# A two-layer decoder trunk: last down product by PSUM bank, final norm in halves

## The chip, the cores and the metric

The kernel runs as one program on one core of a Trainium2 chip. The metric is the device time of one execution in microseconds. The kernel before takes 1856.09 us, the median of three runs (1855.35 to 1857.3).

## The reference

The computation is a causal two-layer decoder trunk on 256 tokens of width 2048, all in float32. Each layer has a token mixer (a pooling mixer in layer 0, differential attention in layer 1) and a SwiGLU feed-forward block, each behind a root-mean-square norm and with a residual addition. A last norm gives the output.

```python
def rmsnorm(x, g, eps=RMS_EPS):
    xf = x.astype(jnp.float32)
    y = xf * lax.rsqrt(jnp.mean(xf * xf, axis=-1, keepdims=True) + eps)
    return (y * g.astype(jnp.float32)).astype(x.dtype)

def swiglu(h, wg, wu, wd):
    return (jax.nn.silu(h @ wg) * (h @ wu)) @ wd

    for i in range(DEPTH):
        ...
        h = h + mix
        h = h + swiglu(rmsnorm(h, norm_ffn[i]), w_gate[i], w_up[i], w_down[i])
    return rmsnorm(h, final_norm)
```

The change touches only the end of the second layer: the last part of the product with `w_down`, its residual addition, and the final `rmsnorm`. The norm needs the sum of squares over all 2048 columns of a token before any column of that token can be scaled.

## The kernel before

**Tiling.** The residual `x_tok` stays in SBUF as two token blocks of 128 rows (t = 0 and 1) by 2048 columns. Weights come in chunks of 1 MB: a `raw` tile of four blocks of 128x512, loaded from SyncE's DMA queue (`load`, L111). ScalarE rounds a chunk to its high half `whi` and VectorE subtracts to get its low half `wlo` (`halves`, L116 to L121). Each float32 product is made of three matmuls, high by high, high by low and low by high (L179). The pools for `raw` and for the halves hold three chunks each.

**A group.** `group` (L142) takes a list of steps, one chunk of weights each, and adds all of them up in PSUM banks. Some steps use a seven-product scheme; the last group of the program uses none (L385: `by_seven` is empty), so each of its six steps has 24 matmuls, six for each of four banks. The banks are C11 (bank 6), C12 (bank 4), C21 (bank 5) and C22 (bank 7); the first digit is the token block and the second the column block of 512. The loop at L158 makes a step's halves and then all of its products, so the steps follow one another and each step visits the four banks in the order C11, C12, C21, C22.

**The feed-forward block.** `ffn` (L351) runs over the hidden dimension in parts of 4, 4 and 3 slices (`CHUNKS`). After each part it multiplies by `w_down`, once for each half `o` of the 2048 output columns. The group of the last part, second layer and o = 1 is the last one of the program: its four banks are the last quarter-columns 1024 to 2047 of both token blocks.

**The end.** For the last group the banks are taken in the order of L389, C11, C12, C21, C22. For each one VectorE adds the bank to the residual (L392), ScalarE squares the 512 new columns with a running sum (L221, the sums in `ss_next`), and VectorE multiplies by the norm's gain into a tile `y` (L398). Behind a token block's second bank, a sum over its four partial sums (L405) and a short chain of 128x1 operations (`rsqrt`, L205: one square root on ScalarE, five small operations on VectorE) give the token's factor. Then the block's four `y` pieces of 512 columns are scaled, two on ScalarE (L408) and two on VectorE (L409), and two DMAs of 512 KB each write 1024 columns each, the first from SyncE's queue, the second from ScalarE's (L410).

**What sets the order.** Each engine has its own queue and works in order. The order within a queue is set at build time by a scheduler of the language's tile layer, from the order in which the program is written and its own costs; waits between engines are semaphores.

Of the kernel before, what the change touches and what calls it, by code (L numbers as in the profile page):

```python
# [9 lines left out]
F32 = mybir.dt.float32  # L10
F32R = mybir.dt.float32r
AF = mybir.ActivationFunctionType
ALU = mybir.AluOpType
AX = mybir.AxisListType
PSUM = bass.MemoryType.PSUM

P = 128
S = 256
D = 2048
# [21 lines left out]
SEVEN_DOWN = (2, 4, 6)  # L41
# [6 lines left out]
A22, A21, A11, A12, S1, S3, S2, S4 = range(8)  # L48
# [4 lines left out]
def trunk_kernel(ctx, tc, x_n, gains, scale_in, final_in, subln, lam_in, band, dist,  # L53
# [10 lines left out]
    nc = tc.nc  # L64
# [5 lines left out]
    tmp = ctx.enter_context(tc.tile_pool(name="tmp", bufs=2))  # L70
# [4 lines left out]
    def bank(i, shape=(P, 512)):  # L75
        return psum.tile(list(shape), F32, name=f"b{i}", tag=f"b{i}")
# [54 lines left out]
    def sum_halves(pool, t):  # L131
        hi = pool.tile([P, 4, 512], F32R, name="thi")
        lo = pool.tile([P, 4, 512], F32R, name="tlo")
        nc.scalar.copy(hi, t)  # L134
        nc.vector.tensor_tensor(lo, t, f32(hi), ALU.subtract)  # L135
        return hi, lo
# [2 lines left out]
    M1, M6, M7, P5, P3, P4, M2, X = range(8)  # L139
    C11, C12, C21, C22 = M2, P3, P4, X  # L140

    def group(steps, pool):  # L142


        plan = []
        for a, seven, src in steps:
            if seven:
                plan.append([(M1, [(A11, 0, B11)]), (M2, [(A12, 0, B21)]), (M6, [(S2, 1, T2)]), (M7, [(S3, 1, T3)]),
                             (P5, [(S1, 1, T1)]), (P3, [(S4, 0, B22)]), (P4, [(A22, 1, T4)])])
            else:  # L150
                plan.append([(C11, [((0, 0), 0, B11), ((1, 0), 0, B21)]), (C12, [((0, 0), 0, B12), ((1, 0), 0, B22)]),
                             (C21, [((0, 1), 0, B11), ((1, 1), 0, B21)]), (C22, [((0, 1), 0, B12), ((1, 1), 0, B22)])])
        left = {}
        for step in plan:
            for b, parts in step:
                left[b] = left.get(b, 0) + 3 * len(parts)
        ps = {}
        for (a, seven, src), step in zip(steps, plan):  # L158
            raw = load(src)
            t = sums(pool, raw) if seven else None  # L160
            w = [halves(raw, B11 if seven else 0)]
            if seven:
                w.append(sum_halves(pool, t))
            for b, parts in step:
                first = b not in ps
                if first:
                    ps[b] = bank(b)
                for at, which, block in parts:
                    hi, lo = w[which]
                    if seven:  # L170
                        ah, al = a[:, 0, at], a[:, 1, at]
                    else:
                        k, t = at
                        if a.shape[2] == 8:
                            slot = ((A11, A21), (A12, A22))[k][t]
                            ah, al = a[:, 0, slot], a[:, 1, slot]
                        else:
                            ah, al = (a[:, k, i, t * P:(t + 1) * P] for i in range(2))
                    for x, y in ((ah, hi), (ah, lo), (al, hi)):  # L179
                        left[b] -= 1  # L180
                        nc.tensor.matmul(ps[b], x, y[:, block], start=first, stop=(left[b] == 0))  # L181
                        first = False
        return ps

    def combined(ps, pool):
# [19 lines left out]
    def rsqrt(ss, n, cols):  # L205


        v, s, t, r = (tmp.tile([P, 8], F32, name=f"rs_{x}") for x in "vstr")
        v, s, t, r = v[:, :cols], s[:, :cols], t[:, :cols], r[:, :cols]
        nc.vector.tensor_scalar(v, ss, 1.0 / n, EPS, ALU.mult, ALU.add)  # L210
        nc.scalar.activation(s, v, AF.Sqrt)
        nc.vector.reciprocal(s, s)
        nc.vector.tensor_tensor(t, s, s, ALU.mult)
        nc.vector.scalar_tensor_tensor(t, t, -0.5, v, ALU.mult, ALU.mult)
        nc.vector.scalar_tensor_tensor(r, t, 1.5, s, ALU.add, ALU.mult)
        return r
# [52 lines left out]
    with tc.tile_pool(name="start", bufs=1, reuse_waits="tile") as st:  # L269
# [78 lines left out]
        residual(2)  # L348
        residual(3)

    def ffn(layer, xq, ss, next_op, next_gain):  # L351

        ss_next = tmp.tile([P, 2, 4], F32, name="ss")
        r = row_scale(ss)
        with tc.tile_pool(name=f"ffn{layer}", bufs=1, reuse_waits="tile") as hp:
            g0 = 0
            ys = []
            for c, n in enumerate(CHUNKS):
                last = c == len(CHUNKS) - 1
                hp_tiles = []  # L360
                if last and next_op is None:
                    final_sb = [hp.tile([P, 1024], F32, name="final_sb", tag=f"h{6 + i}") for i in range(2)]
                    for i in range(2):
                        nc.scalar.dma_start(out=final_sb[i], in_=final_in[:, i * 1024:(i + 1) * 1024])
                for g in range(g0, g0 + n):

                    by_seven = SEVEN[-1:] if g == 0 and layer == 0 else SEVEN
                    cs = combined(group([(xq[p], p in by_seven, w_gu[layer][g, p]) for p in range(NP)], hp), hp)
                    for t in range(2):
                        gate, up = cs[t]  # L370
                        nc.scalar.activation(gate, gate, AF.Silu, scale=r[:, t:t + 1])
                        nc.vector.scalar_tensor_tensor(up, up, r[:, t:t + 1], gate, ALU.mult, ALU.mult)
                    for i in range(2):
                        at = 2 * (g - g0) + i
                        ht = hp.tile(pair_shape(at in SEVEN_DOWN), F32R, name="h", tag=f"h{at}")
                        pair(ht, lambda k, t: cs[t][1][:, (2 * i + k) * P:(2 * i + k + 1) * P], None, at in SEVEN_DOWN)
                        hp_tiles.append(ht)
                for o in range(2):
                    if last and o == 1:

                        pre = tmp.tile([P, 8], F32, name="warm", bufs=1)
                        nc.scalar.activation(pre[:, 0:1], x_tok[:, 0, 0:1], AF.Square)
                        nc.scalar.activation(pre[:, 0:1], pre[:, 0:1], AF.Sqrt)

                    by_seven = () if last and o and next_op is None else SEVEN_DOWN  # L385
                    cs = combined(group([(hp_tiles[i], i in by_seven, w_down[layer][o, 2 * g0 + i])
                                         for i in range(2 * n)], hp), hp)
                    ends = last and o and next_op is None
                    for b, t in ((0, 0), (1, 0), (0, 1), (1, 1)) if ends else ((0, 0), (0, 1), (1, 0), (1, 1)):  # L389
                        j = 2 * o + b  # L390
                        cols = slice(j * 512, (j + 1) * 512)
                        nc.vector.tensor_tensor(x_tok[:, t, cols], cs[t][b], x_tok[:, t, cols], ALU.add)  # L392
                        if last:
                            square_sum(ss_next, t, j)
                        if last and next_op is None:
                            if b == 0 and t == 0:
                                ys.append(hp.tile([P, 2, 2, 512], F32, name="y", tag=("tsum", "thi")[o]))
                            nc.vector.tensor_tensor(ys[o][:, t, b], x_tok[:, t, cols],  # L398
                                                    final_sb[o][:, b * 512:(b + 1) * 512], ALU.mult)
                        if last and t and next_op is not None:  # L400
                            transposed(next_op, j, next_gain, SEVEN_QKV)
                        if ends and b:

                            tot = tmp.tile([P, 2], F32, name="ss_tot")
                            nc.vector.tensor_reduce(tot[:, 0:1], ss_next[:, t], AX.X, ALU.add)  # L405
                            rt = rsqrt(tot[:, 0:1], D, 1)
                            for i in range(2):
                                nc.scalar.activation(ys[i][:, t, 0], ys[i][:, t, 0], AF.Copy, scale=rt)  # L408
                                nc.vector.tensor_scalar(ys[i][:, t, 1], ys[i][:, t, 1], rt, None, ALU.mult)  # L409
                                (nc.scalar if i else nc.sync).dma_start(  # L410
                                    out=out[t * P:(t + 1) * P, i * 1024:(i + 1) * 1024],
                                    in_=ys[i][:, t].rearrange("p b n -> p (b n)"))
                g0 += n
        return ss_next

# [205 lines left out]
```

## Time and profile before

| | |
|---|---|
| median of three runs | 1856.09 us (1855.35 to 1857.3) |
| span of the profiled execution, first to last instruction | 1853.7 us |
| TensorE busy | 1831.7 us, 99% of the span |
| VectorE busy | 1594.9 us, 86% |
| ScalarE busy | 1035.7 us, 56% |
| mean granted TensorE clock | 0.995 |
| output DMAs | four of 512 KB |

No own time is listed for the profiled execution besides its span, so the span stands here for it: the median lies 2.4 us above it (1856.09 less 1853.7). In the views below, PE is TensorE's matmuls, PEld its weight loads, DVE is VectorE, ACT is ScalarE, SPq and ACTq the queues of SyncE and ScalarE when they issue a DMA. A row of the timeline has its start, its length, engine and line, operation, what it writes and reads, and in brackets how long the engine had idled and who released it. A row with x2 merges two neighbours, and the length then covers both.

### The profile page before, as it was taken

How to read it: one execution, taken by the hardware profiler on the slowest of the kernel's cores; microseconds unless marked ns; L12 is line 12 of the kernel's file. 1: busy time of each engine (PE TensorE's matmuls, PEld its weight loads, DVE VectorE, ACT ScalarE, POOL GpSimd, SP SyncE). 2: the span in 40 equal slices, each digit the busy share in tenths (PEclk: the TensorE clock that was granted, in tenths of full speed). 3: DMA queues.
4: the chain of work that ended last, by engine and by line, in shares of the span. 5: the costliest groups of instructions: out<-in, count | busy, mean ns of one | idle time of the engine just before them, and what ended most of it. 6: DMA issues, size and time to landing. Idle time of an engine off the chain costs nothing.

```text
span 1853.7 us, 20951 instructions
## 1 busy us (share of the span) xinstructions
PE 1831.7 (99%) x8250; PEld 1500.6 (81%) x8250; DVE 1594.9 (86%) x1644; ACT 1035.7 (56%) x1001; POOL 0.7 (0%) x6
## 2 busy tenths in 40 slices
PE   7999999999999999999999999999999999999997
PEld 5888888888888888888888888788888888888886
DVE  4789999899898899988878678999889899998985
ACT  4555555555545556656656655555545555545553
POOL 0000000000000000000000000000000000000000
PEclk8999999999999999999999999999999999999999
DMA  6455546555555555555555454555555555566552
GB/s 270 159 192 194 205 170 223 198 194 213 187 212 196 203 190 185 193 182 177 169 173 186 159 182 166 201 205 200 197 212 194 195 202 182 206 226 206 201 190 106
DMA packets 50210, 356.74 MB, mean 192 GB/s; under 512 B 5952, under 2 KB 6080, under 8 KB 7488
## 3 DMA queue, kind: packets, MB, share of 16 engines
q1 hardware_dynamic: 49104, 352.08, 54.4%
q10 hardware_dynamic: 1008, 3.33, 0.5%
q8 instruction: 64, 1.05, 0.2%
q14 instruction: 34, 0.28, 0.1%
HBM read 353.29 MB, written 2.10 MB: 192 GB/s over the span
## 4 chain that ended last, share of the span: by engine, by line
PE 93%; DVE 3%; DMA 1%; ACT 1%; issue 1%; SPq 0%; ACTq 0%; DVEq 0%
PE b L181 88%; PE b L240 2%; DVE wlo L120 1%; PE b L324 1%; PE b L331 1%; PE b L469 1%; DMA band_sb<-band 1%; PE b L499 0%; ACT whi L119 0%; DMA raw<-w_down 0%; PE b L314 0%; DMA raw<-w_v 0%; DVE tsum L125 0%; DMA raw<-w_gu 0%; PE b L315 0%
## 5 line engine op out<-in xcount | busy, mean ns | idle before, releaser
L119 ACT CAST whi<-raw 128x1536 fp32r<-128x1536 f32 (+1 forms) x330 | 585.2, 1774 | 589.1 <-PE b L181 503.5
L181 PE MATMUL b<-whi,xp 128*128 128x512 f32 x2824 | 908.7, 392 | 0.9 <-DVE c L193 0.7
L120 DVE TENSOR_TENSOR wlo<-raw,whi 128x1536 fp32r<-128x1536 f32 (+1 forms) x330 | 697.3, 2113 | 193.6 <-ACT whi L119 193.3
L181 PEld LDWEIGHTS b<-whi,xp 128*128 128x128 f32 x2824 | 528.3, 188 | 110.0 <-DVE c L193 1.2
L181 PE MATMUL b<-wlo,xp 128*128 128x512 f32 x1412 | 551.6, 391 | 0.0
L181 PE MATMUL b<-whi,h 128*128 128x512 f32 x1108 | 354.8, 390 | 0.4 <-DVE c L198 0.4
L181 PEld LDWEIGHTS b<-wlo,xp 128*128 128x128 f32 x1412 | 265.3, 188 | 53.6
L135 DVE TENSOR_TENSOR tlo<-tsum,thi 128x2048 fp32r<-128x2048 f32 x108 | 246.7, 2285 | 3.9 <-ACT thi L134 3.9
L181 PEld LDWEIGHTS b<-whi,h 128*128 128x128 f32 x1108 | 207.5, 188 | 43.8 <-DVE c L198 0.8
L181 PE MATMUL b<-wlo,h 128*128 128x512 f32 x554 | 215.8, 390 | 0.0
L134 ACT CAST thi<-tsum 128x2048 fp32r<-128x2048 f32 x108 | 206.2, 1909 | 14.4 <-DVE tsum L128 14.3
L181 PE MATMUL b<-thi,xp 128*128 128x512 f32 x608 | 211.8, 390 | 0.0
L125 DVE TENSOR_TENSOR tsum<-raw 128x1024 f32<-128x1024 f32 x108 | 131.8, 1220 | 3.6 <-DMA raw<-w_v 1.4
L181 PEld LDWEIGHTS b<-thi,xp 128*128 128x128 f32 x608 | 113.9, 188 | 24.0 <-ACT thi L134 0.9
L181 PEld LDWEIGHTS b<-wlo,h 128*128 128x128 f32 x554 | 104.0, 188 | 21.3
L181 PE MATMUL b<-tlo,xp 128*128 128x512 f32 x304 | 119.5, 393 | 0.0
L181 PE MATMUL b<-thi,h 128*128 128x512 f32 x240 | 83.7, 389 | 0.0
L128 DVE TENSOR_TENSOR tsum<-tsum,raw 128x512 f32<-128x512 f32 x108 | 74.4, 689 | 2.2
L127 DVE TENSOR_TENSOR tsum<-tsum,raw 128x512 f32<-128x512 f32 x108 | 74.0, 685 | 0.7
L181 PE MATMUL b<-whi,oT 128*128 128x512 f32 x236 | 74.4, 392 | 0.0
L181 PEld LDWEIGHTS b<-tlo,xp 128*128 128x128 f32 x304 | 57.1, 188 | 16.0 <-DVE tlo L135 4.3
L181 PEld LDWEIGHTS b<-thi,h 128*128 128x128 f32 x240 | 45.1, 188 | 9.2
(137 smaller groups left out, 1192.9 us busy)
## 6 DMA issues: line engine op xcount, KB each, us to landing
raw<-w_gu SPq DMA_DIRECT2D x176, 1024.0 KB, 4.9
raw<-w_down SPq DMA_DIRECT2D x88, 1024.0 KB, 4.9
raw<-w_qk SPq DMA_DIRECT2D x32, 1024.0 KB, 4.8
raw<-w_v SPq DMA_DIRECT2D x16, 1024.0 KB, 4.9
raw<-w_o SPq DMA_DIRECT2D x16, 1024.0 KB, 4.8
x_tok<-x_n SPq DMA_DIRECT2D x4, 512.0 KB, 7.4
w<-pool_w SPq DMA_DIRECT2D x2, 1024.0 KB, 11.7
raw<-pool_w SPq DMA_DIRECT2D x2, 1024.0 KB, 13.4
```

The source lines that it names most:

```text
L119: nc.scalar.copy(hi[:, lo_block:], raw[:, lo_block:])
L120: nc.vector.tensor_tensor(lo[:, lo_block:], raw[:, lo_block:], f32(hi[:, lo_block:]), ALU.subtract)
L125: nc.vector.tensor_tensor(t[:, T1:T3 + 1], raw[:, B11:B22 + 1], raw[:, B12:B12 + 1].broadcast_to([P, 2, 512]), ALU.add)
L127: nc.vector.tensor_tensor(t[:, T2], t[:, T1], raw[:, B22], ALU.add)
L128: nc.vector.tensor_tensor(t[:, T4], t[:, T2], raw[:, B21], ALU.add)
L134: nc.scalar.copy(hi, t)
L135: nc.vector.tensor_tensor(lo, t, f32(hi), ALU.subtract)
L181: nc.tensor.matmul(ps[b], x, y[:, block], start=first, stop=(left[b] == 0))
L240: nc.tensor.transpose(ps[:, i, 1 - t if seven else t], src(i, t), ident)
L324: nc.tensor.matmul(zp[g][t], a[:, t * P:(t + 1) * P], w[:, at], start=(at == 0), stop=(at == 3))
L331: nc.tensor.matmul(zp[g][t], u, y[:, at], start=(at == 0 and j == 0), stop=(at == 3 and j == 2))
L469: nc.tensor.matmul(sc[:, :nk], qk[:, 0, c, qb * P:(qb + 1) * P], qk[:, 1, c, :nk], start=True, stop=True)
```

## The change

Two things change, both in the last group of the program and behind it.

First, `group` gets a parameter `by_bank`. With 2, which only the last group has, the last two steps are not worked off one after the other: both chunks are prepared, and then for each bank in turn come the six matmuls of the second to last step and the six of the last.

Second, a new function `finish` replaces the end. It takes a token block's two banks in halves of 256 columns: an addition and a squaring for each half, where the first half's squaring need not wait for the second half's addition; the gain multiplication stays at 512 columns. The partial sums of columns 0 to 1023 are summed up ahead of time into a tile `part`. All of one token block's work is written ahead of the other's. Of a block's four scalings one stays on ScalarE and three go to VectorE, and three DMAs write it: 256 KB from ScalarE's queue, then 512 KB and 256 KB from SyncE's.

```diff
-    def group(steps, pool):
+    def group(steps, pool, by_bank=0):
...
+        head = len(steps) - by_bank
+        for (a, seven, src), step in zip(steps[:head], plan[:head]):
+            w = prepared(seven, src)
             for b, parts in step:
...
+                products(a, seven, w, b, parts)
+        if by_bank:
+            ws = [prepared(seven, src) for a, seven, src in steps[head:]]
+            for n in range(len(plan[head])):
+                for (a, seven, src), step, w in zip(steps[head:], plan[head:], ws):
+                    products(a, seven, w, *step[n])
         return ps
...
+    def finish(cs, ys, final_sb, ss):
+
+        for t in range(2):
+            part = tmp.tile([P, 8], F32, name="part", bufs=2)
+            nc.vector.tensor_reduce(part[:, 0:1], ss[:, t, 0:2], AX.X, ALU.add)
+            for b in range(2):
+                for h in range(2):
+                    cols = slice(1024 + b * 512 + h * S, 1024 + b * 512 + (h + 1) * S)
+                    mine = slice(h * S, (h + 1) * S)
+                    nc.vector.tensor_tensor(x_tok[:, t, cols], cs[t][b][:, mine], x_tok[:, t, cols], ALU.add)
+                    sq = tmp.tile([P, 512], F32, name="sq", bufs=1)
+                    at = 1 + 2 * b + h
+                    nc.scalar.activation(sq[:, :S], x_tok[:, t, cols], AF.Square, accum_out=part[:, at:at + 1])
+                cols = slice(1024 + b * 512, 1024 + (b + 1) * 512)
+                nc.vector.tensor_tensor(ys[1][:, t, b], x_tok[:, t, cols], final_sb[1][:, b * 512:(b + 1) * 512], ALU.mult)
+            tot = tmp.tile([P, 2], F32, name="ss_tot")
+            nc.vector.tensor_reduce(tot[:, 0:1], part[:, 0:5], AX.X, ALU.add)
+            rt = rsqrt(tot[:, 0:1], D, 1)
+            rows = slice(t * P, (t + 1) * P)
+            nc.scalar.activation(ys[1][:, t, 0], ys[1][:, t, 0], AF.Copy, scale=rt)
+            nc.scalar.dma_start(out=out[rows, 1024:1536], in_=ys[1][:, t, 0])
+            for b in range(2):
+                nc.vector.tensor_scalar(ys[0][:, t, b], ys[0][:, t, b], rt, None, ALU.mult)
+            nc.sync.dma_start(out=out[rows, 0:1024], in_=ys[0][:, t].rearrange("p b n -> p (b n)"))
+            nc.vector.tensor_scalar(ys[1][:, t, 1], ys[1][:, t, 1], rt, None, ALU.mult)
+            nc.sync.dma_start(out=out[rows, 1536:2048], in_=ys[1][:, t, 1])
...
-                    for b, t in ((0, 0), (1, 0), (0, 1), (1, 1)) if ends else ((0, 0), (0, 1), (1, 0), (1, 1)):
+                    if ends:
+                        finish(cs, ys, final_sb, ss_next)
+                        continue
+                    for b, t in ((0, 0), (0, 1), (1, 0), (1, 1)):
...
-                        if ends and b:
-
-                            tot = tmp.tile([P, 2], F32, name="ss_tot")
-                            nc.vector.tensor_reduce(tot[:, 0:1], ss_next[:, t], AX.X, ALU.add)
-                            rt = rsqrt(tot[:, 0:1], D, 1)
-                            for i in range(2):
-                                nc.scalar.activation(ys[i][:, t, 0], ys[i][:, t, 0], AF.Copy, scale=rt)
-                                nc.vector.tensor_scalar(ys[i][:, t, 1], ys[i][:, t, 1], rt, None, ALU.mult)
-                                (nc.scalar if i else nc.sync).dma_start(
-                                    out=out[t * P:(t + 1) * P, i * 1024:(i + 1) * 1024],
-                                    in_=ys[i][:, t].rearrange("p b n -> p (b n)"))
```

The instruction streams differ only behind the start of the second to last step. TensorE's queue has the same matmuls; before, where the second to last step (its halves `whi_13486` and `wlo_13487`) ends with bank 7 and the last step (`whi_13516` and `wlo_13517`) begins with bank 6, it reads:

```order
L181 MATMUL b7_13387<-whi_13486,h_13106 128x512 x2
L181 MATMUL b7_13387<-wlo_13487,h_13106 128x512
L181 MATMUL b7_13387<-whi_13486,h_13106 128x512
L181 MATMUL b6_13366<-whi_13516,h_13120 128x512 [waits Activation_49]
L181 MATMUL b6_13366<-wlo_13517,h_13120 128x512 [waits DVE_49]
```

And now, with the second to last step's halves as `whi_13487` and `wlo_13488` and the last step's as `whi_13493` and `wlo_13494`:

```order
L184 MATMUL b6_13367<-whi_13487,h_13106 128x512 x2
L184 MATMUL b6_13367<-wlo_13488,h_13106 128x512
L184 MATMUL b6_13367<-whi_13487,h_13106 128x512
L184 MATMUL b6_13367<-whi_13493,h_13120 128x512 [waits Activation_49]
L184 MATMUL b6_13367<-wlo_13494,h_13120 128x512 [waits DVE_49]
```

The last step's first matmul, with its wait for the last chunk's halves, has moved up by 18 matmuls, behind the second to last step's work on bank 6 alone, and each bank's twelve matmuls now stand together.

On VectorE, from the second bank's addition to the scalings of token block 0, the queue before reads (`rs_*` and `ss_tot` are the chain of `rsqrt`; those with `rs_v_13555`, `rs_s_13556`, `rs_t_13557` and `rs_r_13558` belong to block 0, the tile numbers from 13579 on to block 1):

```order
L392 TENSOR_TENSOR x_tok_82<-b7_13387,x_tok_82 128x512 [waits PE_49]
L212 RECIPROCAL rs_s_13556<-rs_s_13556 128x1 [waits Activation_49]
L398 TENSOR_TENSOR y_13547<-x_tok_82,final_sb_12222 128x512 [waits DVE_49]
L213 TENSOR_TENSOR rs_t_13557<-rs_s_13556 128x1 [waits DVE_49]
L405 TENSOR_REDUCE ss_tot_13579<-ss_8667 128x1 [waits Activation_49]
L214 SCALAR_TENSOR_TENSOR rs_t_13557<-rs_t_13557,rs_v_13555 128x1 [waits DVE_49]
L210 TENSOR_SCALAR rs_v_13581<-ss_tot_13579 128x1 [waits DVE_49]
L215 SCALAR_TENSOR_TENSOR rs_r_13558<-rs_t_13557,rs_s_13556 128x1 [waits DVE_49]
L409 TENSOR_SCALAR y_13343<-y_13343,rs_r_13558 128x512 [waits DVE_49]
L409 TENSOR_SCALAR y_13547<-y_13547,rs_r_13558 128x512
L212 RECIPROCAL rs_s_13582<-rs_s_13582 128x1 [waits Activation_49]
```

And now:

```order
L228 SCALAR_TENSOR_TENSOR rs_t_13565<-rs_t_13565,rs_v_13563 128x1 [waits DVE_49]
L229 SCALAR_TENSOR_TENSOR rs_r_13566<-rs_t_13565,rs_s_13564 128x1 [waits DVE_49]
L387 TENSOR_SCALAR y_13343<-y_13343,rs_r_13566 128x512 [waits DVE_49]
L387 TENSOR_SCALAR y_13343<-y_13343,rs_r_13566 128x512
L389 TENSOR_SCALAR y_13344<-y_13344,rs_r_13566 128x512
L374 TENSOR_TENSOR x_tok_82<-b5_13381,x_tok_82 128x256 [waits PE_49]
L374 TENSOR_TENSOR x_tok_82<-b5_13381,x_tok_82 128x256
L379 TENSOR_TENSOR y_13344<-x_tok_82,final_sb_12222 128x512 [waits DVE_49]
L374 TENSOR_TENSOR x_tok_82<-b7_13388,x_tok_82 128x256 [waits PE_49]
L374 TENSOR_TENSOR x_tok_82<-b7_13388,x_tok_82 128x256
L379 TENSOR_TENSOR y_13344<-x_tok_82,final_sb_12222 128x512 [waits DVE_49]
L381 TENSOR_REDUCE ss_tot_13596<-part_13580 128x1 [waits Activation_49]
```

Before, block 0's chain and two of its scalings lay between block 1's last addition (bank 7) and block 1's reciprocal. Now all of block 0's chain and its three scalings stand ahead of block 1's first addition (bank 5), and block 1's chain follows without foreign work in it.

More of the change, by code (lines that the diff above doesn't have):

```diff
@@ L157, in group, with prepared @@
         ps = {}
-        for (a, seven, src), step in zip(steps, plan):
+        def prepared(seven, src):
             raw = load(src)
@@ L163, in group, with products @@
                 w.append(sum_halves(pool, t))
-            for b, parts in step:
[L165 to L182, printed above, removed]
+            return w
+        def products(a, seven, w, b, parts):
+            first = b not in ps
+            if first:
+                ps[b] = bank(b)
+            for at, which, block in parts:
+                hi, lo = w[which]
+                if seven:
+                    ah, al = a[:, 0, at], a[:, 1, at]
+                else:
+                    k, t = at
+                    if a.shape[2] == 8:
+                        slot = ((A11, A21), (A12, A22))[k][t]
+                        ah, al = a[:, 0, slot], a[:, 1, slot]
+                    else:
+                        ah, al = (a[:, k, i, t * P:(t + 1) * P] for i in range(2))
+                for x, y in ((ah, hi), (ah, lo), (al, hi)):
+                    left[b] -= 1
+                    nc.tensor.matmul(ps[b], x, y[:, block], start=first, stop=(left[b] == 0))
+                    first = False
+        head = len(steps) - by_bank
+        for (a, seven, src), step in zip(steps[:head], plan[:head]):
+            w = prepared(seven, src)
+            for b, parts in step:
+                products(a, seven, w, b, parts)
[4 more added lines that the diff above has]
+                    products(a, seven, w, *step[n])
         return ps
@@ L383, in ffn @@
                         nc.scalar.activation(pre[:, 0:1], pre[:, 0:1], AF.Sqrt)
-                    by_seven = () if last and o and next_op is None else SEVEN_DOWN
+                    ends = last and o and next_op is None
+                    by_seven = () if ends else SEVEN_DOWN
                     cs = combined(group([(hp_tiles[i], i in by_seven, w_down[layer][o, 2 * g0 + i])
-                                         for i in range(2 * n)], hp), hp)
-                    ends = last and o and next_op is None
-                    for b, t in ((0, 0), (1, 0), (0, 1), (1, 1)) if ends else ((0, 0), (0, 1), (1, 0), (1, 1)):
+                                         for i in range(2 * n)], hp, 2 if ends else 0), hp)
+                    if ends:
+                        finish(cs, ys, final_sb, ss_next)
+                        continue
+                    for b, t in ((0, 0), (0, 1), (1, 0), (1, 1)):
                         j = 2 * o + b
@@ L396, in ffn @@
                             if b == 0 and t == 0:
-                                ys.append(hp.tile([P, 2, 2, 512], F32, name="y", tag=("tsum", "thi")[o]))
+                                ys.append([hp.tile([P, 2, 2, 512], F32, name="y", tag=("tsum", "thi")[i]) for i in range(2)])
+                                ys = ys[0]
                             nc.vector.tensor_tensor(ys[o][:, t, b], x_tok[:, t, cols],
```

## The prediction

> **What bounds the kernel now.** I read the page's busy table first, then the timeline of the last 35 us for each engine, then the table of stretches around the end.
>
> ```profile
> PE 1831.7 (99%) x8250; PEld 1500.6 (81%) x8250; DVE 1594.9 (86%) x1644; ACT 1035.7 (56%) x1001; POOL 0.7 (0%) x6
> ```
>
> TensorE works 99% of the span, so time before its last matmul can only be won by giving it less to do, and the change gives it the same matmuls. What the change can win lies behind TensorE's last matmul. The table of stretches cuts the end where the trace changes its limit (columns: length, busy time of the engines, granted clock, busy share of the DMA engines, GB/s):
>
> ```profile
> 1832.36:1843.43 11.07, 11.04 (x49) 8.82 (x47) 4.01 (x8) 2.02 (x6) 0.00 (x0) 1.00 0.00 0
> 1843.43:1847.05 3.62, 0.00 (x0) 0.00 (x0) 3.39 (x17) 2.50 (x8) 0.00 (x0) 1.00 0.01 2
> 1847.05:1852.04 4.99, 0.00 (x0) 0.00 (x0) 0.86 (x2) 1.33 (x2) 0.00 (x0) 0.54 1.02 419
> 1852.04:1853.70 1.66, 0.00 (x0) 0.00 (x0) 0.00 (x0) 0.00 (x0) 0.00 (x0) 0.50 0.01 3
> ```
>
> Three limits follow one another. For 3.62 us the norm runs on VectorE and ScalarE while the DMA engines stand idle. Then for 4.99 us the DMA engines are the bound: share 1.02, 419 GB/s, which is the whole output (4.99 us by 419 GB/s is 2.09 MB; four times 512 KB is 2.10). Then 1.66 us pass from the last packet to the end of the program. So the end is set by when the first packet of the output flows and by how many bytes are left then: the chain of waits, which goes through the scalings of block 1, hides that the last transfer stood in line behind the three others. The instructions that lead there:
>
> ```profile
> 1839.35 0.69 DVE L392 TENSOR_TENSOR x_tok<-b,x_tok 128x512 f32<-128x512 f32 x1 [8.00 <-PE b L181]
> ...
> 1840.71 0.69 DVE L392 TENSOR_TENSOR x_tok<-b,x_tok 128x512 f32<-128x512 f32 x1
> ...
> 1842.07 0.69 DVE L392 TENSOR_TENSOR x_tok<-b,x_tok 128x512 f32<-128x512 f32 x1
> ...
> 1843.47 0.68 DVE L392 TENSOR_TENSOR x_tok<-b,x_tok 128x512 f32<-128x512 f32 x1
> ...
> 1845.00 0.16 DVE L405 TENSOR_REDUCE ss_tot<-ss 128x1 f32<-128x4 f32 x1
> ...
> 1845.19 0.15 DVE L210 TENSOR_SCALAR rs_v<-ss_tot 128x1 f32<-128x1 f32 x1
> ...
> 1845.45 0.88 DVE L409 TENSOR_SCALAR y<-y,rs_r 128x512 f32<-128x512 f32 x2
> 1846.25 0.16 DVE L212 RECIPROCAL rs_s<-rs_s 128x1 f32<-128x1 f32 x1
> ...
> 1847.03 0.88 DVE L409 TENSOR_SCALAR y<-y,rs_r 128x512 f32<-128x512 f32 x2
> ```
>
> And in the same stretch on ScalarE, its queue and SyncE's:
>
> ```profile
> 1844.24 0.63 ACT L221 ACTIVATE sq<-x_tok 128x512 f32<-128x512 f32 x1 [0.45 <-DVE rs_s L212]
> 1844.78 0.19 ACT L221 ACTIVATION_READ_ACCUMULATOR sq<-x_tok 128x1 f32 x1
> ...
> 1845.38 0.20 ACT L211 ACTIVATE rs_s<-rs_v 128x1 f32<-128x1 f32 x1 [0.41 <-DVE rs_v L210]
> ...
> 1846.22 2.11 SPq L410 DMA_DIRECT2D out_t<-y  x2
> ...
> 1847.24 1.33 ACT L408 ACTIVATE y<-y,rs_r 128x512 f32<-128x512 f32 x2 [0.43 <-DVE rs_r L215]
> 1848.60 0.35 ACTq L410 DMA_DIRECT2D out_t<-y  x1
> ```
>
> The four additions start 1.36 us apart, as the last step finishes its four banks, six matmuls each; a matmul thus takes 1.36/6 = 0.227 us. Block 0 has its factor only at 1845.4, and its first packet flows at 1847.05, 0.83 us behind the issue at 1846.22.
>
> **The change, part by part.**
>
> *Work by bank.* The matmuls stay the same; the banks now end 12 matmuls apart, 2.72 us instead of 1.36. Counted back from the last bank's end at 1843.43 (1842.07 + 1.36), they end at 1835.27, 1837.99, 1840.71 and 1843.43: both banks of block 0 end earlier by 4.08 and 2.72 us, block 1's first by 1.36, the last not at all. The price could be a wait of TensorE for the last chunk, since the last step now starts 18 matmuls (4.08 us) sooner. Its last matmul starts at 1843.01, so its first, 23 before, at 1837.80; now that one comes at 1833.72.
>
> ```profile
> 1827.11 1.91 ACT L119 CAST whi<-raw 128x2048 fp32r<-128x2048 f32 x1 [3.53 <-PE b L181]
> ...
> 1829.06 2.29 DVE L120 TENSOR_TENSOR wlo<-raw,whi 128x2048 fp32r<-128x2048 f32 x1 [3.15 <-ACT whi L119]
> ...
> 1843.01 0.39 PE L181 MATMUL b<-whi,h 128*128 128x512 f32 x1
> ```
>
> The last chunk's low half is ready at 1831.35, 2.37 us ahead of that. The cast at 1827.11 waited for TensorE to leave the buffer of three steps before, which the change does not move. So I cost this at nothing; every microsecond by which the low half came later than 1833.72 would cost one. The two small reductions that now stand ahead of the last two low halves on VectorE (0.16 us each) fall into its idle time.
>
> *Block 0 under the matmuls.* Sizes for halves come from lines of the attention with the same shape, grouped by form:
>
> ```profile
> L471 DVE TENSOR_TENSOR s_sb<-b,bias 128x256 f32<-128x256 f32 x16 | 6.7, 416 | 0.0
> ...
> L519 ACT ACTIVATE sq<-b 128x256 f32<-128x256 f32 x16 | 6.2, 385 | 0.5 <-PE b L515 0.4
> ...
> L519 ACT ACTIVATION_READ_ACCUMULATOR sq<-b 128x1 f32 x16 | 3.2, 202 | 0.0
> ```
>
> A half addition takes 0.42 us and the next follows about 0.33 behind it; a half squaring with its read of the sum takes about 0.5 (0.385 and 0.202, overlapping by 0.1 as at full width). Block 0's second bank at 1837.99: second half added at 1838.74, its squaring done at 1839.5, the sum at 1839.55. From a sum to the first scaling the chain costs 1.39 us: 0.19 to `rs_v` (1845.00 to 1845.19), 0.19 to the root, 0.23 for the root, and 0.78 from reciprocal to scaling (1846.25 to 1847.03). So the factor serves at 1840.95. Three scalings follow 0.40 apart (two took 0.88, one alone 0.48) and end at 1842.2. ScalarE scales its piece by 1841.7. Block 0's three transfers are issued from 1841.7 to 1842.3, and its 1 MB has left by about 1842.5 + 2.5 = 1845.0, on DMA engines that were idle (share 0.00 up to 1843.43).
>
> *What queues behind it.* Block 1's first bank, ready at 1840.71, stands on VectorE behind block 0's scalings and waits until 1842.1. Its halves and its gain product take till 1843.5, where the next instruction may start; the last bank is ready at 1843.43, so this costs it 0.1 us.
>
> *Block 1.* Halves at 1843.5 and 1843.85, the second done at 1844.3; the squarings end at about 1845.0, as before (the read that starts at 1844.78 ends at 1844.97). Splitting wins nothing here: the two reads of the sum and the late start eat it. The sum starts at 1845.06 (before 1845.00). The chain of 1.39 us now runs without block 0's two scalings, which kept the reciprocal waiting from 1845.6, the root's end, to 1846.25. First scaling at 1846.45 instead of 1847.03: 0.58 us won. ScalarE scales one piece, half of 1.33 and some (0.71), and issues at 1847.25; SyncE issues 512 KB at 1847.4 and 256 KB at 1847.8. The last issue was at 1848.60. SyncE's last transfer also waits for a load's completion that was cast long before; that costs nothing.
>
> *The transfers.* 0.83 us behind the first issue packets flow, at 1848.08. Only 1 MB is left, 1.05 MB / 419 GB/s = 2.50 us, so the last packet is at 1850.6 and the end 1.66 us later at 1852.24. Against 1853.70 that is -1.46 us. The unknown is a 256 KB transfer with rows of 2 KB, which the trace does not have. From below its time goes with the bytes (0.62 us), from above it takes as long as one of 512 KB (1.25 us); two of them then make the stage 1.26 us longer, and the gain 0.2. I take the lower, since the stretch at 419 GB/s shows no gap between transfers, and shade the sum to **-1.4 us**. The span would be 1852.3 and the median, which lies 2.4 us above the span, 1856.09 - 1.4 = **1854.7 us**, or 0.08% faster.
>
> By the Trainium skill, page "DMA: Bandwidth & Descriptors", section "Bandwidth" (its measured table), transfers should be batched to 1 MiB, as smaller ones reach a smaller part of the peak: 6.15 us for 1 MB and 0.95 us for 64 KB. An estimate drawn straight between these, one transfer after another, gives block 1 some 7.4 us in three transfers against 6.8 in two, so the split would cost 0.6. That rule speaks against the change; here four transfers of 512 KB in 4.99 us, 1.25 us each, are far below the table, and I keep the row.
>
> **The rivals.**
>
> *Block 0's chain delays block 1 (slower).* In the trace of before, block 0 took 4.74 us from its second bank's addition (1840.71) to its first scaling (1845.45), not the 2.96 I sum up, because other work lay in between. If the work that now overlaps it (two halves, gain product, squarings in line) kept it that long, the third scaling would end at 1844.0, block 1's last bank would be added at 1845.4 instead of 1843.5, and the end is 1.9 us later than forecast: +0.5 us, 1856.6. It turns to a loss where block 0's chain is 1.4 us longer than I sum. Against it: VectorE's queue has only block 0 in it there.
>
> *The extra transfers each pay their own start.* SyncE's 512 KB landed 3.0 us after issue (median), of which 1.25 is bytes:
>
> ```profile
> out_t<-y SPq DMA_DIRECT2D x2, 512.0 KB, 3.0
> ```
>
> If block 1's third transfer did not overlap, that is 1.75 us more than forecast, +0.3 us, 1856.4. Against it: four transfers ran back to back at share 1.02, and these are issued within 0.6 us. The page's rule above is of this kind.
>
> *The closing part shrinks too.* The 1.66 us behind the last packet contain a landing behind 2 MB of queued writes; if it fell by 0.5, the time would be 1854.2. For it: less in the queue. Against: the engines' closing work is in it too.
>
> *The change does nothing.* If TensorE waited for the last chunk after all by 1.4 us, the gain is gone: 1856.1. The slack of 2.37 us speaks against it.
>
> **How the numbers follow.** Forecast 0.74, block 0's delay 0.07, transfers 0.09, shorter closing 0.07, no effect 0.03. All lie within 0.2% of 1856.09 (3.7 us, about what a measurement can tell from no change). A gain beyond that would need a time below 1852.4, more than the whole 3.62 us of the norm's stretch; a loss needs 1859.8. Only the spread of runs and a shift of the whole program are left for these: faster 0.05, slower 0.03, same 0.92. The cases go from 1854.2 to 1856.6; the three runs lie 0.7 below to 1.2 above their median, so the range is 1853.3 to 1856.7.
>
> **What would show it.** In the profile after: additions of 256 columns at about 1835.3, 1838.0, 1842.1 and 1843.5 (the third late behind three scalings); no idle time of TensorE in the last 11 us; DMA busy in two stretches, about 1842.5 to 1845 and 1848.1 to 1850.6, with idle time between; first scaling of block 1 near 1846.45; the span's end 1.66 us behind the last packet. I am wrong if TensorE's last matmul moves, if the second stretch is longer than 2.7 us, or if block 1's sum starts later than 1845.3.

## The result, and the profile after

The changed kernel takes 1873.21 us (median of 4 runs, 1872.33 to 1873.72) against 1856.69 us for the kernel before (1855.35 to 1857.58). The ratio is 1.0092, with a 95% interval of 1.008 to 1.0105: 16.5 us slower by the medians, where the prediction had 1.4 us faster and a range up to 1856.7.

From the head of the profile after:

```profile
span 1871.3 us, 20967 instructions
...
PE 1852.1 (99%) x8250; PEld 1503.0 (80%) x8250; DVE 1599.3 (85%) x1652; ACT 1035.0 (55%) x1007; POOL 0.7 (0%) x6
```

TensorE has the same 8250 matmuls and is busy for 20.4 us more (1852.1 less 1831.7). The loss thus lies where TensorE works and not behind its last matmul. Its clock is not the reason: the mean granted clock is 0.995 in both profiles. The chain of waits shows where it lies. Each of its rows has a start, a length, and the work; those with 547 matmuls in a row are the feed-forward stages. Of the kernel before:

```profile
232.45 124.36 PE b L181 x547
...
1572.08 124.36 PE b L181 x547
```

And of the changed kernel:

```profile
234.31 126.46 PE b L184 x547
...
1586.87 126.46 PE b L184 x547
```

The same 547 matmuls take 2.1 us more, already 234 us into the program, and by the same amount in the last such stage: 124.36/547 is 0.2273 us a matmul, 126.46/547 is 0.2312. The first of them is some 1600 us ahead of the first changed instruction. In a matmul one operand is stationary (128x128, loaded ahead of it by a weight load, a row of PEld) and the other is the moving operand (128x512). Here the moving operand is `whi`, `wlo`, `thi` or `tlo`, halves of the weight chunks (`thi` and `tlo` those of sums of their blocks, for the seven-product scheme), and the stationary one is `xp`, `h` or `oT`, the activations. Grouped by form, the matmuls whose stationary operand is `h` or whose moving operand is `thi` have grown. Before:

```profile
L181 PE MATMUL b<-whi,h 128*128 128x512 f32 x1108 | 354.8, 390 | 0.4 <-DVE c L198 0.4
...
L181 PE MATMUL b<-thi,xp 128*128 128x512 f32 x608 | 211.8, 390 | 0.0
```

And in the changed kernel:

```profile
L184 PE MATMUL b<-whi,h 128*128 128x512 f32 x1108 | 361.4, 397 | 0.0
...
L184 PE MATMUL b<-thi,xp 128*128 128x512 f32 x608 | 214.9, 395 | 0.0
```

The largest group, `whi` by `xp`, has 392 ns before and 393 now. These lengths overlap, so the pitch, from the start of one matmul to the start of the next, says it more directly (means in ns over all such matmuls of the trace, stalls left out, worked out from their start times):

| moving, stationary | matmuls | before | after |
|---|---|---|---|
| `whi`, `xp` | 2680 | 227.2 | 228.4 |
| `wlo`, `xp` | 1360 | 227.2 | 227.4 |
| `whi`, `h` | 1080 | 226.9 | 233.4 |
| `wlo`, `h` | 550 | 227.1 | 233.3 |
| `thi`, `xp` | 606 | 227.0 | 232.3 |
| `tlo`, `xp` | 294 | 227.2 | 229.7 |
| `thi`, `h` | 240 | 227.0 | 228.9 |
| `whi`, `oT` | 230 | 227.3 | 233.4 |

What the groups that grew most have in common is that the place of an operand in SBUF has changed. The new tile `part` has 8 columns of float32 in two buffers, 64 bytes of each partition, in the pool `tmp`. In the built program's layout all pools behind `tmp` stand 64 bytes further than before: `h0` at 178240 instead of 178176, `thi` at 153664 instead of 153600, `tlo`, `oT` and the small tiles of the first layer too. `xp`, `raw`, `whi` and `wlo` lie ahead of `tmp` and have not moved.

The end itself did what was forecast. The table of stretches of the changed kernel, from the first packet of block 0 on:

```profile
1861.31:1864.04 2.73, 0.95 (x5) 0.42 (x3) 2.54 (x6) 2.04 (x8) 0.00 (x0) 1.00 0.98 384
1864.04:1866.90 2.86, 0.00 (x0) 0.00 (x0) 2.09 (x9) 0.93 (x2) 0.00 (x0) 0.83 0.00 0
1866.90:1869.79 2.89, 0.00 (x0) 0.00 (x0) 0.00 (x0) 0.00 (x0) 0.00 (x0) 0.50 0.93 363
1869.79:1871.27 1.48, 0.00 (x0) 0.00 (x0) 0.00 (x0) 0.00 (x0) 0.00 (x0) 0.50 0.00 0
```

The output now goes out in two pieces with an idle time of the DMA engines between them. TensorE's last matmul starts at 1861.86 and ends at 1862.26, so the end takes 9.0 us; before it was 10.3 (1843.01 + 0.39 to 1853.7).

### The profile page after: what moved, and what is told of

It reads as the page before. It is cut to its first block, busy times and chain, and to the rows that moved or that the text cites. A ratio compares the mean times of both kernels' runs of the same rounds, so it can differ in the third digit from the quotient of the medians.

```text
span 1871.3 us, 20967 instructions
## 1 busy us (share of the span) xinstructions
PE 1852.1 (99%) x8250; PEld 1503.0 (80%) x8250; DVE 1599.3 (85%) x1652; ACT 1035.0 (55%) x1007; POOL 0.7 (0%) x6
## 4 chain that ended last, share of the span: by engine, by line
PE 96%; DVE 2%; DMA 1%; ACT 1%; issue 0%; SPq 0%; DVEq 0%; ACTq 0%
PE b L184 90%; PE b L254 2%; PE b L338 1%; PE b L345 1%; PE b L503 1%; DMA band_sb<-band 1%; DVE wlo L120 0%; PE b L533 0%; PE b L328 0%; DMA raw<-w_gu 0%; PE b L329 0%; DVE tlo L135 0%; PE b L549 0%; DVE tsum L125 0%; PE b L547 0%
## 5 line engine op out<-in xcount | busy, mean ns | idle before, releaser
L184 PE MATMUL b<-whi,h 128*128 128x512 f32 x1108 | 361.4, 397 | 0.0
```

## The experiments

Two theories stood against each other: that the matmuls are slow because their operands moved in SBUF, and that the new instructions, or their place in the program, slow TensorE. The kernels that are called the kernel before with a tile moved keep its instructions and change only where tiles lie; the others keep those of the changed kernel, or of one part of it.

**The changed kernel with a shift of 128 bytes.**

```diff
-            part = tmp.tile([P, 8], F32, name="part", bufs=2)
+            part = tmp.tile([P, 16], F32, name="part", bufs=2)
```

> The changed kernel with one size doubled: the tile part has 16 columns instead of 8, so its two buffers take 128 bytes of a partition instead of 64, and every tile laid out behind them (thi, tlo, h, oT, mean_hl) stands 128 bytes further than before instead of 64. The instructions are the same as in the changed kernel. Theory A (the matmuls are slower because their operands moved by 64 bytes): the pitch of the matmuls is that of before again, 0.227 us, and only the gain at the end is left, 1.2 us (from the last matmul to the end 9.0 us instead of 10.3): 1855.4. Rival B (the new instructions themselves, their placement in the instruction stream or the new order of the last matmuls, slow TensorE): as changed, 1873.

Measured: 1872.35 us against 1855.37, ratio 1.0089 (1.0074 to 1.0104). This is the time that the rival gave, and theory A as it was put before the run, for which a shift of 128 bytes should have cost nothing, is refuted. The pitches are slow as well: `whi` by `h` is at 232.3 ns instead of 233.4, and `thi` by `xp` at 232.8 instead of 232.3. So either the place is not the cause or 128 bytes are about as bad as 64; this run alone cannot tell.

**The kernel before, moved by 64 bytes.**

```diff
-        r = tmp.tile([P, 2], F32, name="r_tok", bufs=3)
+        r = tmp.tile([P, 2], F32, name="r_tok", bufs=5)
```

> The kernel before with nothing changed but the number of buffers of r_tok, the last tile laid out ahead of the large ones, from 3 to 5: 64 bytes more, every instruction as before. Theory A: 17 to 18 us slower, 1874, with whi by h at a pitch near 233.5 ns instead of 227. Rival B: 1856.7 as before.

Measured: 1874.31 us, ratio 1.0099 (1.0082 to 1.0115). The tile has only three uses in the program, so the added buffers change no wait, and the built instructions are those of before; still the whole loss is there without one line of the change. A row of its chain:

```profile
233.92 126.46 PE b L181 x547
```

It is the changed kernel's 126.46. This refutes the rival: the loss needs none of the new instructions.

**The kernel before with only the stationary operands moved.**

```diff
-        m1, u2, u3, p5 = (pool.tile([P, 512], F32, name=f"c{i}") for i in ("11", "12", "21", "22"))
+        m1, u2, u3 = (pool.tile([P, 512], F32, name=f"c{i}") for i in ("11", "12", "21"))
+        p5 = pool.tile([P, 528], F32, name="c22")[:, 0:512]
```

> The kernel before, where only the stationary operands h and oT (and what lies behind them) move by 64 bytes: the tile c22 is laid out 16 columns wider and used as before. whi, wlo, thi, tlo and xp stay. If a 64 byte offset of the stationary operand against the moving one is enough (A1), the products with h and oT, some 2400 matmuls, cost 6.3 ns more each, 15 us: 1871, and those with xp keep 227 ns. If what counts is that the moving halves thi and tlo lie at 64 (A2), nothing: 1856.7. Rival B: 1856.7.

Measured: 1867.96 us, ratio 1.0066 (1.0051 to 1.0081), 12.6 us where 15 were expected. Products with `h` are at 233 ns whatever the moving operand is (`whi` 233.4, `thi` 233.1), those with `xp` at 227 (`whi` 227.2, `thi` 227.1). So moving the stationary operand is enough: `whi` by `h` has grown, `thi` by `xp` has the 390 ns of before:

```profile
L181 PE MATMUL b<-whi,h 128*128 128x512 f32 x1108 | 361.2, 396 | 0.0
...
L181 PE MATMUL b<-thi,xp 128*128 128x512 f32 x608 | 211.7, 390 | 0.0
```

**The kernel before with all operands moved together.**

```diff
-    gain_sb = const.tile([P, 6, NK], F32, name="gain_sb")
+    gain_sb = const.tile([P, 7, NK], F32, name="gain_sb")
...
-        nc.scalar.dma_start(out=gain_sb, in_=gains)
+        nc.scalar.dma_start(out=gain_sb[:, 0:6], in_=gains)
```

> The kernel before, where the gain tile at the very front is 64 bytes larger, so that all operands of all matmuls, moving and stationary, move by 64 bytes together. If each address has to be a multiple of 128 bytes on its own (A3): all 8100 matmuls cost 6.3 ns more, 51 us: 1907. If only the offset between the two operands of a matmul counts (A4): 1856.7, or at most the 2 ns that the few products of thi with h showed, in which both had moved, 16 us: 1873. Rival B: 1856.7.

Measured: 1855.76 us, ratio 0.9998 (0.9989 to 1.0008). Now `h`, `thi`, `xp`, `whi` and the operands of all other matmuls stand 64 bytes further, and nothing is lost:

```profile
233.18 124.37 PE b L181 x547
```

So no address is bad by itself. What counts is the distance between two operands.

**The period.** With the layouts of all runs so far I sorted the matmuls by the address of the stationary operand that is loaded for the next matmul (the expectation below calls it the weights), less the address of the matmul's own moving operand. For all but 11 of some 7340 such matmuls of the changed kernel the distance to the matmul's own stationary operand is the same, so the sorting does not tell the two apart. The kernel before has only distances that are multiples of 256, and 227 ns at all of them; groups at 64, 128 and 192 bytes off such a multiple have means of 229.7 to 233.5. That asks for a shift of 256 in the changed kernel.

```diff
-            part = tmp.tile([P, 8], F32, name="part", bufs=2)
+            part = tmp.tile([P, 32], F32, name="part", bufs=2)
```

> The changed kernel with the tile part at 32 columns, so that all tiles behind it stand 256 bytes further than before; instructions as in the changed kernel. The runs so far leave this theory: a matmul is at 227 ns where the address of the weights loaded for the next matmul, less that of its own moving operand, is a multiple of 256 bytes, and at 232 to 233 ns where it is 64, 128 or 192 off. Then the pitch is that of before and the gain at the end shows alone: 1854.2, 1.2 us under the 1855.4 that before had beside the last runs. Rival (any move of these tiles costs, or a larger period than 256): 1868 to 1874.

Measured: 1854.08 us against 1855.57, ratio 0.9992 (0.9983 to 1.0001). The loss is gone with 24 more unused columns in a small tile, though all the new instructions are there:

```profile
232.71 124.34 PE b L184 x547
```

**The kernel before, offset by offset.** Each tile of `h` and `oT` is moved by an amount of its own.

```diff
+    H_AT = (0, 16, 32, 64, 96, 128, 192, 224)
+    O_AT = (4, 80, 48, 40, 32, 16, 88, 160)
+
+    def placed(pool, seven, off, name, tag, more):
+        shape = pair_shape(seven)
+        n = shape[1] * shape[2] * shape[3]
+        whole = pool.tile([P, n + more], F32R, name=name, tag=tag)
+        return whole[:, off // 4:off // 4 + n].rearrange("p (a b c) -> p a b c", a=shape[1], b=shape[2])
...
-                        ht = hp.tile(pair_shape(at in SEVEN_DOWN), F32R, name="h", tag=f"h{at}")
+                        ht = placed(hp, at in SEVEN_DOWN, H_AT[at], "h", f"h{at}", 64)
...
+                oT[h] = placed(op_, h in SEVEN_O, O_AT[h], f"oT{h}", f"oT{h}", 40)
```

> The kernel before with each tile of h and oT laid out at its own offset: h0 to h7 at 0, 16, 32, 64, 96, 128, 192 and 224 bytes, oT0 to oT7 at 4, 240, 112, 8, 160, 48, 24 and 256 bytes off a multiple of 256, while whi, wlo, thi, tlo and xp stay. By the theory of a period of 256 the pitch is 227 ns at 0 and 256 and 232 to 234 ns at 64, 96, 128, 160, 192. Whether it is a step (any offset costs) or a ramp (4 to 48 and 224 to 240 cost less) is open; a step gives 1867, as with h and oT moved by 64. If an offset should be faster than 0, it shows here as a pitch under 226.

Measured: 1865.22 us, a single execution, so the time has no interval; what counts here are the pitches. The pitch of `whi` by these tiles, by the distance modulo 256:

| distance, bytes | 0 | 4 | 8 | 16 | 24 | 32 | 48 | 64 | 96 | 112 | 128 | 160 | 192 | 224 | 240 |
|---|---|---|---|---|---|---|---|---|---|---|---|---|---|---|---|
| pitch, ns | 227 | 233 | 230.5 | 230 | 230 | 233 | 233 | 234 | 234 | 233 | 232 | 235 | 231 | 233 | 227 |

The value at 0 is that of `oT7`; `h0`, at distance 0 too, has a mean of 228.5 with a median of 227; why its mean is higher is not shown. Neither a step nor a ramp describes the row: 8 to 24 bytes and 192 cost about half, 240 costs nothing, 4 costs nearly all (24 matmuls only). No distance is faster than 0.

**The work by bank alone, and the new end alone.** The first has `group` as changed and the old end; the second is the changed kernel at a shift of 256 with this edit:

```diff
-                                         for i in range(2 * n)], hp, 2 if ends else 0), hp)
+                                         for i in range(2 * n)], hp, 0), hp)
```

> The kernel before with the last two steps worked off by bank and the old end behind it (no halves, two scalings on each engine, two transfers of 512 KB for each block); no tile moves. From the last matmul's end to the end of the span 10.3 us before and 9.0 with the whole change. Block 0 finishes under the matmuls here too, and block 1's chain is free of it: last bank at 1843.4, sum at 1844.95, first scaling 1846.35, first packet of block 1 1848.15, end 1852.3: 8.9 us. So theory A, that the work by bank alone brings the gain: 9.0. Rival, that halves and three scalings on VectorE bring it: 10.

> The changed kernel with the tiles 256 bytes further, but with the last group's steps one after the other as before. Block 0's banks come at 1839.35 and 1840.71, its chain and its three scalings last till about 1845.0 and stand ahead of block 1's additions on VectorE, so block 1's last bank is added at 1846.2 instead of 1843.5: 11.7 us from the last matmul's end to the end, 1.4 us more than before. Rival, that the new end helps by itself: 9.5 to 10.

Measured: by bank alone 1854.47 us (ratio 0.9991, 0.9981 to 1.0002), the new end alone 1855.74 (0.9998, 0.9988 to 1.0008). The times can't tell them apart; the profiles can, counted from the last matmul's end. Three stretches each: from there to block 1's first packet (in the new end alone, to the first packet of all), while the output flows, and behind it. Of the changed kernel at a shift of 256:

```profile
1842.90:1847.69 4.79, 0.00 (x1) 0.00 (x0) 3.85 (x13) 2.24 (x8) 0.00 (x0) 1.00 0.38 152
1847.69:1850.46 2.77, 0.00 (x0) 0.00 (x0) 0.00 (x0) 0.00 (x0) 0.00 (x0) 0.56 0.95 378
1850.46:1852.02 1.56, 0.00 (x0) 0.00 (x0) 0.00 (x0) 0.00 (x0) 0.00 (x0) 0.50 0.00 0
```

Of the work by bank with the old end:

```profile
1843.81:1848.38 4.57, 0.00 (x0) 0.00 (x0) 3.22 (x10) 2.29 (x6) 0.00 (x0) 1.00 0.37 150
1848.38:1851.02 2.64, 0.00 (x0) 0.00 (x0) 0.00 (x0) 0.00 (x0) 0.00 (x0) 0.54 0.97 396
1851.02:1852.47 1.45, 0.00 (x0) 0.00 (x0) 0.00 (x0) 0.00 (x0) 0.00 (x0) 0.50 0.00 0
```

Of the new end without the work by bank:

```profile
1843.39:1847.06 3.67, 0.00 (x1) 0.00 (x0) 3.60 (x16) 2.24 (x9) 0.00 (x0) 1.00 0.00 1
1847.06:1852.83 5.77, 0.00 (x0) 0.00 (x0) 1.56 (x5) 0.72 (x1) 0.00 (x0) 0.65 0.96 363
1852.83:1854.28 1.45, 0.00 (x0) 0.00 (x0) 0.00 (x0) 0.00 (x0) 0.00 (x0) 0.50 0.00 0
```

That is 9.12, 8.66 and 10.89 us against 10.27 before (3.62, 4.99 and 1.66). The gain of the end comes from the work by bank, 1.6 us; halves, three scalings on VectorE and three transfers for each block, taken together, cost 0.5 us on top of it and 0.6 without it. Without it the cost lies in the transfers: the whole output flows for 5.77 us at 363 GB/s where before it took 4.99 at 419. The second expectation (11.7) was too high: here the scheduler placed block 1's additions ahead of block 0's scalings again, so they did not wait.

Where the new end loses on top of the work by bank can be read behind the last matmul, which ends at 1842.91 in the changed kernel at a shift of 256 and at 1843.81 in the other. In the first the sum comes 1.77 us later, in the second 1.58:

```profile
1844.68 0.16 DVE L381 TENSOR_REDUCE ss_tot<-part 128x1 f32<-128x5 f32 x1
```

```profile
1845.39 0.16 DVE L419 TENSOR_REDUCE ss_tot<-ss 128x1 f32<-128x4 f32 x1
```

The 1 MB of block 1 leaves in 2.77 us in three transfers, in 2.64 in two, and the stretch behind the last packet is 1.56 us against 1.45. Which part of the new end costs what was not tried one by one.

**Both measured again.** The two kernels once more, unchanged.

> The work by bank with the old end once more, for an interval and a second profile, beside the changed kernel with its tiles 256 bytes further. In the first profile it took 8.66 us from the last matmul's end to the end (before 10.27). If that is no accident: again 8.6 to 8.8, and 1.6 us less than before.

> The changed kernel with its tiles 256 bytes further, once more beside it: 9.0 to 9.1 us from the last matmul's end to the end and 1.2 us less than before; the 0.4 us that the halves and the scalings cost against the old end is under what the times can tell, and is read from the profiles alone.

Measured: by bank with the old end 1853.76 us against 1855.68, ratio 0.999 (0.9981 to 0.9998); the changed kernel at a shift of 256 1854.47, ratio 0.9997 (0.9988 to 1.0006). From the last matmul to the end they take 8.67 and 9.12 us, within 0.01 us of the first profiles. The work by bank with the old end, which needs no new tile, has the lowest median here, 1.9 us under before, and its interval just excludes no change; that of the other does not, and the two intervals overlap. That it is the better of the two rests on the profiles of the end.

## Why the prediction was wrong

**The step that failed** is in its first part, below the busy table: "time before its last matmul can only be won by giving it less to do, and the change gives it the same matmuls". The same matmuls did not take the same time. The change was costed instruction by instruction; the tile `part` enters the sum through its two reductions alone, put at nothing because they fall into idle time, and its place in SBUF was not considered. Its 64 bytes move every tile of the later pools, and about 3300 matmuls with a moved operand take up to 6.5 ns more each on the mean, 233.4 ns for `whi` by `h` instead of 226.9. From the pitches, counts by differences give 7.0 us for `whi` by `h`, 3.4 for `wlo` by `h`, 3.2 and 0.7 for `thi` and `tlo` by `xp`, 2.0 for `oT` (1.4 for `whi`, 0.6 for `wlo`), 0.9 for `thi` and `tlo` by `h`, and 3.2 for `whi` by `xp`, whose own operands did not move: 20.4 us, as much as TensorE's busy time grew. That last term belongs to matmuls that stand behind moved ones: the `whi` and `wlo` by `xp` that come as the first to the seventh matmul behind one with a moved operand have mean pitches of 227.9 to 236.1 ns, the eighth and those behind it (up to the 24th) 227.0 or less; in the kernel before the first seven have 226.7 to 226.9. The last matmul ends 18.9 us later (1862.26 less 1843.40); the difference is idle time of TensorE that shrank ahead of it (22.0 - 10.3 = 11.7 us before, 19.2 - 9.0 = 10.2 after).

**The chances** followed the step: slower, of which a shift of the whole program was one source, got 0.03, without a mechanism or a price. The trace of before has only one layout and could show nothing of another. The first point from which the prediction called itself wrong, a last matmul that moves, is what happened. No rival had it.

**The end, point by point**, counted from the last matmul's end:

| | predicted | changed kernel |
|---|---|---|
| additions of block 0 | -8.1, -5.4 | -8.4, -5.6 |
| additions of block 1 | -1.3, +0.1 | -1.4, 0.0 |
| sum of block 1 | +1.66 | +1.64 |
| first scaling of block 1 | +3.05 | +3.03 |
| first packet of block 1 | +4.68 | +4.64 |
| length of its transfers | 2.50 | 2.89 |
| from last packet to end | 1.66 | 1.48 |
| end | +8.84 | +9.01 |

- *Work by bank without a wait of TensorE*: right. VectorE's last low half is done at 1849.73 in the changed kernel (1847.44 + 2.29). The first matmul of the last step comes 41 matmuls ahead of the last one, at about 1852.3 (1861.86 - 41 x 0.2333), so 2.6 us later; TensorE waits for nothing there.

```profile
1847.44 2.29 DVE L120 TENSOR_TENSOR wlo<-raw,whi 128x2048 fp32r<-128x2048 f32 x1 [3.31 <-ACT whi L119]
```

- *Block 0's scalings delay block 1's first addition*: right. The bank is ready twelve matmuls ahead of the last one's end, at about 1859.5 (1862.26 less 2.8), and is added at 1860.89. *The last bank by 0.1*: not seen. It is added at 1862.30, 0.04 us behind the last matmul's end, as in the work by bank with the old end, where VectorE stood ready (1843.85 and 1843.81).

```profile
1860.49 0.48 DVE L389 TENSOR_SCALAR y<-y,rs_r 128x512 f32<-128x512 f32 x1
1860.89 0.75 DVE L374 TENSOR_TENSOR x_tok<-b,x_tok 128x256 f32<-128x256 f32 x2
```

- *The transfers*: mis-sized by 0.4 us. The 1 MB in three transfers takes 2.89 us at 363 GB/s instead of 2.50 at 419, over the 2.7 that was named as a sign of error. At a shift of 256 the same three take 2.77, and two transfers of 512 KB take 2.64 (by bank alone), so between 0.1 and 0.25 us of it go with the smaller transfers; the rest is also there with two transfers of 512 KB, and its cause is open.
- *The closing part*: 0.2 us shorter, some third of the 0.5 that the rival on it gave. Its reason, less in the queue, is not borne out: in the new end alone, where the whole output flows in one stretch, the closing part is as short, 1.45 us.
- *The rival on block 0's chain* did not come: from the second bank's addition to the first scaling its chain takes 3.00 us (1856.70 to 1859.70) where 2.96 were summed. *The rival on unoverlapped transfers*, +1.75 us, did not come either.

With the shift at a multiple of 256 the kernel takes 1.5 us less than before by the medians (1854.08 and 1855.57) and 1.2 when measured again, near the sum for the end (1.4); both intervals still contain no change. The profiles show the end itself shorter by 1.15 us (10.27 less 9.12).

## What to carry to other kernels

A new tile, however small, is an edit to the layout of every tile behind it; compare the addresses of the two built programs before calling the rest of a kernel unchanged, and pad a new tile so that the distances between matmul operands stay as they were; here a shift of 256 bytes cost nothing and one of 64 or 128 did cost. Where a profile shows a change in stages that were not edited, read the pitch of the same instructions grouped by operand before reading the edit. An edit in two parts may owe its gain to one of them: here the order of the last matmuls gave 1.6 us and the rewritten end took 0.5 of it back.

## What the runs showed of the hardware

In these kernels, with a new stationary operand loaded for each matmul, the pitch of back-to-back 128x512 float32r matmuls depends on the distance in a partition between the moving and the stationary operand: 227 ns where it is a multiple of 256 bytes, 230 to 235 ns at most other distances tried, 227 again at 240. Matmuls at distance 0 are slow too, up to 236 ns, within seven places behind slow ones in the changed kernel. The Trainium skill, page "SBUF — State Buffer", section "Who interferes with whom", gives TensorE two read ports for SBUF, one for the moving operand and one for the weight load, independent of each other. By that the place of one operand relative to the other would not matter for the rate. The runs do not agree: with all operands moved together nothing changes (ratio 0.9998), with the stationary operands `h` and `oT` alone moved by 64 bytes the time grows by 0.66%.

What stays open is why. A shared resource that both reads meet, with a period of 256 bytes, would look like this, but no run here shows the reads themselves. Nor is it told apart whether the distance to the next stationary operand counts or that to the matmul's own. The few matmuls of the changed kernel in which the two differ speak against the next one alone: six whose next stationary operand is 64 bytes off and whose own is at 0 stay at 225.5 ns, and five the other way round are at 234.2. But with a shift of 128 bytes the same six are at 232.5.
